# Gated linear attention in a decoder trunk: split logits and norms, Silu from Exp and Ln, heads closed at other points, another bank for the first key

## The chip, the cores and the metric

The kernel runs on one core of a Trainium2 chip. The time is the device time of one execution in microseconds (us), lower is better; three runs of the kernel before gave a median of 1874.64 us (1874.52 to 1875.6). Engines are named as in the profile: PE is the matrix engine and PEld its weight loads, DVE the vector engine, ACT the scalar engine (activation functions), POOL the general-purpose engine, SP the engine whose queue issues the weight DMAs. The matrix engine's results land in PSUM, eight banks of 128 partitions x 512 fp32; everything else lives in SBUF.

## The reference

512 tokens of width 1024 pass two layers. Each layer is a half-step SwiGLU, a mixer, another half-step SwiGLU, all behind RMSNorms. Layer 0 mixes by gated linear attention (GLA), layer 1 by stick-breaking attention. The change is in the GLA mixer only:

```
proj = h @ w_in                                  # q 512, k 512, v 1024, g 1024, gk_lr 16 columns
log_a = log_sigmoid(gk_lr @ w_gk2 + b_gk) / 16   # (512, 512): the gate logits
b = cumsum(log_a)                                # per chunk, 4 heads x 128 channels
o = sum over s <= t of (q_t * exp(b_t - b_s) * k_s) v_s       # per head, 256 wide
o = rmsnorm(o, o_norm)                           # per head, over its 256 channels
y = (o * silu(g)) @ w_out
```

## The kernel before, in words

**Precision.** Nearly every product is made of parts. A tensor is cut into a high part (ACT copies it to fp32r, a form of fp32 that the matrix engine takes in one pass) and a low part (DVE subtracts the high part), and `mm3` (L66) adds high x high, low x high and high x low. The weights are cut the same way (L124 on ACT, L126 on DVE). Some products are plain fp32 instead, which the trace shows as two matmul records for each: the gate logits `ps_z<-w,ga` (L776), the cumulative sums `ps_d<-tri,la` (L789), all products inside a head, and the output norms' sums `ps_on<-osq,gT` (L908), where a column of ones in `gT` is broadcast as the stationary operand.

**The feed.** All weight products of the whole trunk stand in one list of entries (`feed.q`), each with its weights' DMA, their cutting and a generator of matmul groups. The phases pull groups from it (`feed.step`, `feed.entries`) and put their own work between. `Feed.start` cuts weights up to three entries ahead, into four buffers each of `wh` and `wl`, and loads up to six ahead on SP's queue. The order on each engine is finally set by the planner of the language, from costs of its own; it moves instructions past each other where the data allow, and where the kernel says `issue_after` it keeps that order.

**The GLA phase** (`GLA.run`, L945). `two_halves` runs q of heads 0 and 1 (kept in PSUM, `defer`, because the RMSNorm's factor `R` isn't there yet), `stats_a` makes the row sums, `gate_low` (L763) the 16 gate columns (`ps_gk`), `stats_b` (L391) broadcasts `R` (`ps_R`, then the copy L405). Then `flush` evacuates q0 and q1 (L721), `gate_logits` (L769) scales the gate columns (L770), makes the four logit tiles (L776), and takes log-sigmoid as Abs, Exp, Ln on ACT (L778 to L780) and min-minus on DVE (L781) into `la`. Two entries, k0 and k1, follow; then `decay` (L786) makes b of heads 0 and 1.

PSUM is shared out by tags: two banks "a", three "z", two "t", one "o". All features of the mixer (q, k, g; L702, L705, L713) and v use "a"; "o" holds the small transposes, state updates and norm sums of a head.

Then come four heads. `levels(h)` (L793) builds the 128 x 128 decayed scores of head h in seven halvings: for each, DVE forms two differences of b (L811, L812), ACT takes Exp, DVE multiplies k and q on (L814, L815), PE multiplies (`ps_S`, L839) and DVE copies under a mask into `S` (L840). `output(h)` (L850), interleaved with the levels of the next head, decays the keys (`kd`), transposes them (`ps_kd`), updates the states (`ps_s`, L880 to L887), makes the output (`ps_o`), squares it (L901, L905), sums it over 256 channels by the product with ones (`ps_on`), and computes 1/rms as Exp(-0.5 Ln) with a correction step (L910 to L920) and the scaled output `on` (L924). One feed step stands between any two steps of these.

The eight gate features g are evacuated as `gn = ps * R` (L736) as they come; in the program, Silu on them (`silu`, L930) stands after all features of the phase and is followed by the load of the activation table that has Exp and Ln (L427). Only then `close(g)` (L936) is called for heads 0, 1 and 2: `on * gn`, cut into `oh` and `ol`; head 3 is closed at the end. The last two entries (`back`, L227, body L260) are the product with `w_out`: two halves of four output tiles each, where the parts of head 3 (`late=2`) come last in each half.

The gate weights are set up at the phase's start on POOL (`gate_weights`, L738): `w2` is zeroed, `w_gk2` is loaded twice, the bias once at partition 64 beside a row of ones in `ga`.

Of the kernel before, what the change touches and what calls it, by code (L numbers as in the profile page):

```python
# [10 lines left out]
F32 = mybir.dt.float32  # L11
# [21 lines left out]
def decoder(ctx: ExitStack, tc: tile.TileContext, a: dict, out: bass.AP):  # L33
# [100 lines left out]
    class Feed:  # L134
# [17 lines left out]
            e = self.q[i]  # L152
            return e.body(e.W)

        def step(self, n=1):
            while n > 0:
                if self.cur is None:
                    self.cur = self.start()
                if next(self.cur, self) is self:
                    self.cur = None  # L160
                else:
                    n -= 1
# [21 lines left out]
    def feat(ch, f, evac, tag=None, defer=None):  # L184


        def body(W):
            (wh, wl), = W
            ps = psum("ps_f", tag)
            for part in (range(0, KD // 2), range(KD // 2, KD)):  # L190
                for k in part:
                    mm3(ps, wh[:, k], wl[:, k], st["h"][k], st["l"][k], k == 0, k == KD - 1)
                if part[-1] == KD - 1:
                    if defer is None:
                        evac(ps)
                    else:
                        defer.append((evac, ps))
                yield

        feed.q.append(Entry([(ch, lambda t: t[:, :, f * P : (f + 1) * P], KD, P)], body))  # L200
# [492 lines left out]
    class GLA:  # L693
        def __init__(self, w_in, w_gk2, b_gk, og, w_out, nxt):
            self.w_in, self.w_gk2, self.b_gk, self.og = w_in, w_gk2, b_gk, og
            self.defer = []
            self.q, self.k, self.b, self.v = [None] * 4, [None] * 4, [None] * 4, []
            self.gn, self.on, self.hs = [None] * KD, [None] * KD, []
            chunks = [Chunk(cols(w_in, c * 256, 256), KD, 256) for c in range(4)]

            def qk(h):
                feat(chunks[h // 2], h % 2, lambda ps: self.evac_q(h, ps), "a", self.defer if h < 2 else None)  # L702

            def kk(h):
                feat(chunks[2 + h // 2], h % 2, lambda ps: self.evac_k(h, ps), "a")  # L705

            qk(0), qk(1), kk(0), kk(1), qk(2), qk(3), kk(2), kk(3)
            for c in range(4):
                tok(w_in, 1024 + c * 256, lambda i, ps, c=c: self.evac_v(c, i, ps), "a")
            for c in range(4):  # L710
                ch = Chunk(cols(w_in, 2048 + c * 256, 256), KD, 256)
                for f in range(2):
                    feat(ch, f, lambda ps, j=2 * c + f: self.evac_g(j, ps), "a")  # L713
            back(w_out, 0, KD, self.hs, 1.0, nxt, late=2, tags=("a", "a", "z", "z", "z", "t", "t", "o"))
# [19 lines left out]
        def evac_g(self, j, ps):  # L734
            self.gn[j] = self.gp.tile([P, T], F32, tag="g", name="gn")
            nc.vector.tensor_tensor(out=self.gn[j], in0=ps, in1=st["R"], op=ALU.mult)  # L736

        def gate_weights(self):  # L738

            gr = self.ep.tile([P, KD, 16], F32, tag="gr", bufs=1, name="gr")  # L740
            with nc.allow_non_contiguous_dma("gate columns"):
                nc.gpsimd.dma_start(gr, cols(self.w_in, 3072, 16))
            self.gs = gs = self.ep.tile([P, KD, P], F32R, tag="gs", bufs=1, name="gs")
            nc.gpsimd.memset(gs.bitcast(F32), 0.0)
            nc.scalar.copy(gs[:, :, 0:16], gr)
            nc.vector.tensor_tensor(
                out=gs[:, :, 32:48], in0=gr, in1=gs[:, :, 0:16].bitcast(F32), op=ALU.subtract
            )
            self.w2 = w2 = self.gp.tile([P, T], F32, tag="g", name="w2")
            nc.gpsimd.memset(w2, 0.0)  # L750
            nc.gpsimd.dma_start(w2[0:16], self.w_gk2)
            nc.gpsimd.dma_start(w2[32:48], self.w_gk2)
            nc.gpsimd.dma_start(w2[64:65], self.b_gk)
            self.tri = self.ep.tile([P, P], F32, tag="tri", bufs=1, name="tri")
            nc.gpsimd.dma_start(self.tri, a["c_tri"])
            lf = self.ep.tile([P, len(LEVELS) * P // 2], F32, tag="e", name="lf")
            nc.gpsimd.dma_start(lf, a["c_lvl"])
            self.lvl = self.ep.tile([P, len(LEVELS) * P // 2], U8, tag="lvl", bufs=1, name="lvl")
            nc.vector.tensor_copy(self.lvl, lf)
            self.ga = self.gp.tile([P, T], F32, tag="g", name="ga")  # L760
            nc.gpsimd.memset(self.ga[64:65], 1.0)

        def gate_low(self):  # L763
            self.psg = psum("ps_gk", "z")
# [2 lines left out]
                mm(self.psg, self.gs[:, k], st["l"][k], False, k == KD - 1)  # L767

        def gate_logits(self):  # L769
            nc.vector.tensor_tensor(  # L770
                out=self.ga[0:64], in0=self.psg[0:64], in1=st["R"][0:64], op=ALU.mult
            )
            self.la = []
            for i in range(NT):
                ps = psum("ps_z", "z")
                mm(ps, self.ga[0:65, i * P : (i + 1) * P], self.w2[0:65], True, True)  # L776
                t = self.gp.tile([P, T], F32, tag="g", name="la")
                nc.scalar.activation(t, ps, AF.Abs)  # L778
                act(t, t, AF.Exp, scale=-1.0)
                act(t, t, AF.Ln, bias=1.0)  # L780
                nc.vector.scalar_tensor_tensor(  # L781
                    out=t, in0=ps, scalar=0.0, in1=t, op0=ALU.min, op1=ALU.subtract
                )
                self.la.append(t)
# [65 lines left out]
        def output(self, h):  # L850
# [40 lines left out]
            for vb in range(2):  # L891
                ps = psum("ps_o", "t")
                c0 = h * 256 + vb * P
                for i in range(NT):
                    s = slice(i * P, (i + 1) * P)
                    mm(ps[:, s], v[i][:, c0 : c0 + P], S[:, i], True, i == 0)
                    if i > 0:
                        mm(ps[:, s], sts[i - 1][:, vb * P : (vb + 1) * P], eb[:, s], False, True)
                po.append(ps)
                t = ep.tile([P, T], F32, tag="e", name="osq")  # L900
                nc.scalar.activation(t, ps, AF.Square)  # L901
                if vb == 0:
                    sq = t
                else:
                    nc.vector.tensor_tensor(out=sq, in0=sq, in1=t, op=ALU.add)  # L905
                yield
            ps = psum("ps_on", "o")
            mm(ps, ones, sq, True, True)  # L908
            vv = ep.tile([P, T], F32, tag="e", name="vv")
            nc.vector.tensor_scalar(  # L910
                out=vv, in0=ps, scalar1=1.0 / 256, scalar2=EPS, op0=ALU.mult, op1=ALU.add
# [15 lines left out]
                self.on[j] = t  # L927
            yield

        def silu(self):  # L930
            for j in range(KD):
                with tc.issue_after(st["last"]):
                    s = nc.scalar.activation(self.gn[j], self.gn[j], AF.Silu).ins
            exp_ln_tables(s)

        def close(self, h):  # L936
            for j in (2 * h, 2 * h + 1):
                nc.vector.tensor_tensor(out=self.on[j], in0=self.on[j], in1=self.gn[j], op=ALU.mult)
                hh = self.gp.tile([P, T], F32R, tag="g", name="oh")
                hl = self.qp.tile([P, T], F32R, tag="q", name="ol")  # L940
                nc.scalar.copy(hh, self.on[j])
                nc.vector.tensor_tensor(out=hl, in0=self.on[j], in1=hh.bitcast(F32), op=ALU.subtract)
                self.hs.append((hh, hl))

        def run(self):  # L945
            with ExitStack() as es:
# [17 lines left out]
                self.decay(0)  # L964
                self.decay(1)
                prev = None
                for h in range(4):
                    if h == 1:
                        self.decay(2)
                        self.decay(3)  # L970
                    for n, _ in enumerate(self.levels(h)):
                        feed.step(1)
                        if prev is not None and n >= 1:
                            next(prev, None)
                            if n == 4:
                                feed.step(1)
                    if prev is not None:
                        for _ in prev:
                            feed.step(1)
                    prev = self.output(h)  # L980
                    if h == 3:
                        while feed.pos < self.end:
                            feed.step(1)
                        feed.finish()
                        next(prev)
                        self.silu()
                        for g in range(3):
                            self.close(g)
                for n, _ in enumerate(prev):
                    if n < 6:  # L990
                        feed.step(1)
                self.close(3)
                feed.entries(self.end + 2 - feed.pos)


# [331 lines left out]
```

## Time and profile before

| what | value |
|---|---|
| three timed runs, median | 1874.64 us |
| the profiled execution, time | 1874.33 us |
| the profiled execution, span from first to last instruction | 1872.2 us |
| granted TensorE clock | 0.998 |
| PE busy, share of span | 1847.3 us, 99% |
| DVE busy | 1412.0 us, 75% |
| ACT busy | 1012.5 us, 54% |
| POOL busy | 7.3 us |
| DMA, mean over the span | 96 GB/s |

The profile is of one execution. Its time is 2.1 us more than its span, and 0.3 us under the median of the runs. The GLA phase lies between about 354 us (the first q product) and 598 us (the first product of the next SwiGLU) of the span. "Chain of waits" below means the profile's chain of work that ended last, shown in order of time: start, length, what ran. A group line gives line, engine, operation, result and operands, shapes and count, then busy time and mean ns of one, then the idle time before.

### The profile page before, as it was taken

The numbers are of one execution on the slowest core, as the hardware profiler recorded it, in microseconds if no ns is written. First come the engines' busy times: TensorE is split into PE (matmuls) and PEld (weight loads), VectorE is DVE, ScalarE is ACT, GpSimd is POOL, SyncE is SP. The second block draws the span as 40 slices with busy tenths as digits, with TensorE's granted clock in tenths as the row PEclk, the third lists the DMA queues.
The fourth block names the chain that finished last, engine by engine and source line by source line (L and its number), as shares of the span: only waits on it lengthen the run. The fifth ranks groups of instructions, "written<-read, shape, count | busy, mean of one in ns | idle before, by whom it ended". The sixth has DMA issues, their size and how long they took to land.

```text
span 1872.2 us, 29140 instructions
## 1 busy us (share of the span) xinstructions
PE 1847.3 (99%) x11933; PEld 1650.8 (88%) x11933; DVE 1412.0 (75%) x2177; ACT 1012.5 (54%) x1714; POOL 7.3 (0%) x17
## 2 busy tenths in 40 slices
PE   8999999999999999999999999999999999999998
PEld 6899999789888899999888999998888788999997
DVE  7977776775767987777788777676878769777775
ACT  6544545444555554454555545445878755554454
POOL 0000000100000000000000000000000000000000
PEclk9999999999999999999999999999999999999999
DMA  5433333212123233342233333233221223333321
GB/s 158 130 107 110 105 113 103 87 48 66 61 75 113 79 102 102 107 129 80 79 113 116 111 102 113 79 92 101 68 68 57 68 90 113 102 102 102 119 85 68
DMA packets 177513, 179.04 MB, mean 96 GB/s; under 512 B 4034, under 2 KB 167924, under 8 KB 177380
## 3 DMA queue, kind: packets, MB, share of 16 engines
q1 hardware_dynamic: 176768, 176.18, 30.0%
q8 instruction: 93, 1.52, 0.3%
q0 software_dynamic: 512, 0.99, 0.2%
q14 instruction: 40, 0.33, 0.1%
q10 hardware_dynamic: 100, 0.03, 0.0%
HBM read 175.11 MB, written 2.10 MB: 95 GB/s over the span
## 4 chain that ended last, share of the span: by engine, by line
PE 88%; DVE 9%; ACT 1%; issue 1%; DMA 0%; SPq 0%; DVEq 0%; ACTq 0%
PE ps_d L64 25%; PE ps_w L523 20%; PE ps_f L64 11%; PE ps_q L523 10%; PE ps_z L523 5%; PE ps_t L64 5%; PE ps_b L64 4%; DVE wl L126 2%; PE ps_S L64 1%; PE ps_z L1058 1%; PE ps_bt L64 1%; DVE ts L615 1%; DVE xn L599 1%; DVE nl L606 1%; PE ps_oT L1120 1%; PE ps_T L1105 1%
## 5 line engine op out<-in xcount | busy, mean ns | idle before, releaser
L126 DVE TENSOR_TENSOR wl<-raw,wh 128x1024 fp32r<-128x1024 f32 x244 | 259.9, 1066 | 96.6 <-ACT wh L124 61.5
L124 ACT CAST wh<-raw 128x1024 fp32r<-128x1024 f32 x244 | 224.7, 923 | 131.2 <-PE ps_f L64 44.4
L64 PE MATMUL ps_d<-hh,wl 128*128 128x512 f32 x672 | 262.4, 390 | 0.0
L64 PE MATMUL ps_d<-hh,wh 128*128 128x512 f32 x672 | 262.3, 390 | 0.0
L64 PE MATMUL ps_d<-hl,wh 128*128 128x512 f32 x672 | 261.6, 389 | 0.0
L523 PE MATMUL ps_w<-th,wl 128*128 128x256 f32 x864 | 239.1, 277 | 5.0 <-DVE wl L126 5.0
L523 PE MATMUL ps_w<-tl,wh 128*128 128x256 f32 x864 | 239.0, 277 | 0.9 <-DVE tl L606 0.9
L523 PE MATMUL ps_w<-th,wh 128*128 128x256 f32 x864 | 239.2, 277 | 0.2
L307 DVE SCALAR_TENSOR_TENSOR x<-ps_d,x 128x512 f32<-128x512 f32 x184 | 124.9, 689 | 115.9 <-PE ps_d L64 115.6
L126 DVE TENSOR_TENSOR wl<-s,wh 128x1024 fp32r<-128x1024 f32 x144 | 176.1, 1223 | 40.7 <-PE ps_z L523 19.3
L124 ACT CAST wh<-s 128x1024 fp32r<-128x1024 f32 x144 | 151.2, 1050 | 93.2 <-PE ps_q L523 30.0
L124 ACT CAST wh<-rawd 128x1024 fp32r<-128x1024 f32 x84 | 88.4, 1053 | 201.7 <-issue 98.9
L64 PE MATMUL ps_f<-xh,wh 128*128 128x512 f32 x448 | 182.1, 407 | 1.6 <-DVE q L721 1.5
L64 PE MATMUL ps_f<-xl,wh 128*128 128x512 f32 x448 | 175.5, 392 | 0.0
L64 PE MATMUL ps_f<-xh,wl 128*128 128x512 f32 x448 | 175.0, 391 | 0.0
L523 PEld LDWEIGHTS ps_w<-th,wl 128*128 128x128 f32 x864 | 162.3, 188 | 5.8 <-DVE wl L126 5.8
L523 PEld LDWEIGHTS ps_w<-tl,wh 128*128 128x128 f32 x864 | 162.2, 188 | 1.1 <-DVE tl L606 1.1
L523 PEld LDWEIGHTS ps_w<-th,wh 128*128 128x128 f32 x864 | 162.2, 188 | 1.0 <-ACT wh L124 1.0
L64 PEld LDWEIGHTS ps_d<-hl,wh 128*128 128x128 f32 x672 | 126.2, 188 | 26.7
L64 PEld LDWEIGHTS ps_d<-hh,wh 128*128 128x128 f32 x672 | 126.2, 188 | 24.5
L64 PEld LDWEIGHTS ps_d<-hh,wl 128*128 128x128 f32 x672 | 126.2, 188 | 23.8
L126 DVE TENSOR_TENSOR wl<-rawd,wh 128x1024 fp32r<-128x1024 f32 x84 | 102.9, 1225 | 53.6 <-ACT wh L124 40.1
(248 smaller groups left out, 4434.4 us busy)
## 6 DMA issues: line engine op xcount, KB each, us to landing
raw<-in_ffn_w_gate_dram SPq DMA_DIRECT2D x43, 1024.0 KB, 5.3
raw<-in_ffn_w_up_dram SPq DMA_DIRECT2D x43, 1024.0 KB, 5.4
rawd<-in_ffn_w_down_dram SPq DMA_DIRECT2D x84, 512.0 KB, 3.5
raw<-in_gla_w_in_dram SPq DMA_DIRECT2D x12, 1024.0 KB, 5.5
raw<-in_sb_w_in_dram SPq DMA_DIRECT2D x16, 512.0 KB, 3.8
raw<-in_gla_w_out_dram SPq DMA_DIRECT2D x4, 1024.0 KB, 5.0
raw<-in_sb_w_in_dram SPq DMA_DIRECT2D x4, 1024.0 KB, 5.3
raw<-in_sb_w_out_dram SPq DMA_DIRECT2D x4, 1024.0 KB, 5.0
```

The costliest lines, as they stand in the source:

```text
L64: st["pe"] = nc.tensor.matmul(ps, l, r, start=first, stop=last).ins
L124: st["cut"] = nc.scalar.copy(h, r).ins
L126: nc.vector.tensor_tensor(out=l, in0=r, in1=h.bitcast(F32), op=ALU.subtract)
L307: nc.vector.scalar_tensor_tensor(out=xs[k], in0=ps, scalar=0.5, in1=xs[k], op0=ALU.mult, op1=ALU.add)
L523: st["pe"] = nc.tensor.matmul(o, l_, r_, start=first and j + n == 0, stop=j == 3 and n == 2, skip_group_check=True).ins
L599: nc.vector.scalar_tensor_tensor(out=t, in0=xs[k], scalar=g, in1=st["R"], op0=ALU.mult, op1=ALU.mult)
L606: nc.vector.tensor_tensor(out=l, in0=t, in1=h.bitcast(F32), op=ALU.subtract)
L615: nc.vector.tensor_tensor(out=o, in0=p, in1=q, op=ALU.subtract)
L1058: nc.tensor.matmul(o_, l_, r_, start=first, stop=last, skip_group_check=True)
L1105: nc.tensor.transpose(ps[:, c0 : c0 + P], ys[yb][:, yc + j * P : yc + (j + 1) * P], ident)
L1120: nc.tensor.matmul(po[e * 64 : e * 64 + 64, j * P : T], self.v[j][:, c : c + 64], self.wt[p, e][bk][:, c0 : c0 + n], start=j == 0, stop=j ...
```

## The change

Four edits, all in `class GLA` but for one argument in `Feed.step`.

1. **First key.** k0 takes the bank "o" instead of an "a".
2. **Logits by parts.** `w2` is copied to fp32r on 128 partitions (`w2r`): w_gk2 four times, the bias at two partitions; the last 32 partitions hold the low part (ACT copy, DVE subtraction). `ga` becomes fp32r with high part, low part and high part again, so that one product of 128 partitions gives high x high, low x high and high x low. It is made by one DVE product (`gl`), an ACT copy, a DVE subtraction and another ACT copy, where one DVE product made it before. POOL zeroes/sets whole tiles and issues six DMAs for `w2` where it issued three.
3. **Norm sums by parts.** The squares are cut into `sh` (ACT) and `sl` (DVE), and two fp32r products with a ones column of fp32r replace one fp32 product.
4. **Silu and closing.** Each g feature gets its Silu right after its evacuation, as g * exp(min(g, 0) - ln(1 + exp(-|g|))): Abs, Exp, Ln on ACT, one DVE operation, Exp on ACT, one DVE product. `silu()` with its table switch goes. A head is closed as soon as its output and its two gates are there, checked after each feed step of the phase, with the feed stopped at the phase's last entries until then.

The diff, cut to its core:

```diff
@@ Feed
-        def step(self, n=1):
+        def step(self, n=1, end=None):
             while n > 0:
                 if self.cur is None:
+                    if self.pos == end:
+                        return
                     self.cur = self.start()
@@ GLA
-                feat(chunks[2 + h // 2], h % 2, lambda ps: self.evac_k(h, ps), "a")
+                feat(chunks[2 + h // 2], h % 2, lambda ps: self.evac_k(h, ps), "o" if h == 0 else "a")
...
             nc.vector.tensor_tensor(out=self.gn[j], in0=ps, in1=st["R"], op=ALU.mult)
+            s = self.ep.tile([P, T], F32, tag="s", bufs=2, name="sg")
+            nc.scalar.activation(s, self.gn[j], AF.Abs)
+            act(s, s, AF.Exp, scale=-1.0)
+            act(s, s, AF.Ln, bias=1.0)
+            nc.vector.scalar_tensor_tensor(
+                out=s, in0=self.gn[j], scalar=0.0, in1=s, op0=ALU.min, op1=ALU.subtract
+            )
+            act(s, s, AF.Exp)
+            nc.vector.tensor_tensor(out=self.gn[j], in0=self.gn[j], in1=s, op=ALU.mult)
+            self.gates = j + 1
...
-            nc.gpsimd.dma_start(w2[0:16], self.w_gk2)
-            nc.gpsimd.dma_start(w2[32:48], self.w_gk2)
-            nc.gpsimd.dma_start(w2[64:65], self.b_gk)
+            for r in range(0, P, 32):
+                nc.gpsimd.dma_start(w2[r : r + 16], self.w_gk2)
+            for r in (48, 112):
+                nc.gpsimd.dma_start(w2[r : r + 1], self.b_gk)
+            self.w2 = self.gp.tile([P, T], F32R, tag="g", name="w2r")
+            nc.scalar.copy(self.w2, w2)
+            low = slice(96, P)
+            nc.vector.tensor_tensor(out=self.w2[low], in0=w2[low], in1=self.w2[low].bitcast(F32), op=ALU.subtract)
+            one = self.ep.tile([P, 64], F32R, tag="one", bufs=1, name="one")[:, 0:1]
+            nc.scalar.copy(one, gT[:, 50:51])
+            self.ones = one.to_broadcast([P, P])
...
-            nc.vector.tensor_tensor(
-                out=self.ga[0:64], in0=self.psg[0:64], in1=st["R"][0:64], op=ALU.mult
-            )
+            ga, t = self.ga, self.ep.tile([P, T], F32, tag="e", name="gl")
+            nc.vector.tensor_tensor(out=t[0:48], in0=self.psg[0:48], in1=st["R"][0:48], op=ALU.mult)
+            nc.scalar.copy(ga[0:48], t[0:48])
+            nc.vector.tensor_tensor(out=ga[64:80], in0=t[0:16], in1=ga[0:16].bitcast(F32), op=ALU.subtract)
+            nc.scalar.copy(ga[96:112], t[0:16])
...
-                mm(ps, self.ga[0:65, i * P : (i + 1) * P], self.w2[0:65], True, True)
+                mm(ps, ga[:, i * P : (i + 1) * P], self.w2, True, True)
...
+            nc.scalar.copy(sh, sq)
+            nc.vector.tensor_tensor(out=sl, in0=sq, in1=sh.bitcast(F32), op=ALU.subtract)
             ps = psum("ps_on", "o")
-            mm(ps, ones, sq, True, True)
+            mm(ps, self.ones, sh, True, False)
+            mm(ps, self.ones, sl, False, True)
...
+        def step(self, n=1):
+            feed.step(n, self.end)
+            self.close_ready()
+
+        def close_ready(self):
+            while self.closed < min(self.outs, self.gates // 2):
+                self.close(self.closed)
+                self.closed += 1
@@ GLA.run, head 3
                     if h == 3:
+                        next(prev)
                         while feed.pos < self.end:
-                            feed.step(1)
+                            self.step()
                         feed.finish()
-                        next(prev)
-                        self.silu()
-                        for g in range(3):
-                            self.close(g)
+                        self.close_ready()
```

`feed.step(1)` becomes `self.step()` everywhere in the loop over heads, `self.outs` counts the heads whose output is complete, and the last `self.close(3)` becomes `self.outs = 4` and `close_ready()`. The full order on each engine, as built, is known for both kernels: on PE it is the same before the GLA phase and from the next SwiGLU on.

## The prediction

> **What bounds the kernel now.** I read the page first, then the chain of waits over the GLA phase, the matrix engine's own waits, and the busy times by stage.
>
> ```profile
> PE 1847.3 (99%) x11933; PEld 1650.8 (88%) x11933; DVE 1412.0 (75%) x2177; ACT 1012.5 (54%) x1714; POOL 7.3 (0%) x17
> ```
>
> PE is never free, so a saving on another engine is worth nothing by itself: the time falls by PE work removed and by PE waits removed, and rises by new waits. The chain over the phase's head shows both kinds:
>
> ```profile
> 369.61 0.91 PE ps_R L401 x8
> ...
> 370.54 0.70 DVE R L405
> ...
> 371.26 0.70 DVE q L721
> ...
> 372.01 1.67 PE ps_f L64 x6
> 373.68 2.58 PE ps_z L64 x6
> 376.26 1.38 PE ps_f L64 x6
> 377.64 1.10 PE ps_z L64 x2
> 378.74 8.19 PE ps_f L64 x36
> 386.93 1.78 PE ps_d L64 x16
> ```
>
> From 370.51 to 372.01 PE stands still: k0 needs an "a" bank, and both hold q0 and q1 until L721. Then four logits take 2.58 + 1.10 = 3.68 us, two records each (0.46 us a record in this chain), while the 36 fp32r products take 8.19 / 36 = 0.2275 each. PE's waits of the whole span that lie in this phase:
>
> ```profile
> PE ps_f L64 <- DVE q L721: 1.5, 1, 1.5
> ...
> PE ps_o L64 <- DVE on L924: 0.6, 1, 0.6
> PE ps_b L64 <- ACT oh L941: 0.6, 1, 0.6
> ```
>
> The last two stand at 546 and 549 us, where heads 0 to 2 are closed late. For the stretch from the first g product to there (columns: length, then busy PE, PEld, DVE, ACT, POOL):
>
> ```profile
> 481.62:546.00 64.38, 64.34 (x355) 54.03 (x353) 41.75 (x79) 39.72 (x51) 0.00 (x0) 1.00 0.21 66
> ```
>
> PE is full; DVE has 22.6 us to spare, ACT 24.7. The clock column is 1.00 and DMA 0.21, so neither is in play.
>
> **The change, part by part.** The base is the profiled execution's 1874.33 us (span 1872.2 + 2.1), 0.3 under the median of the runs.
>
> *First key and logits.* In the order as built, PE goes from the gate columns through one k0 product and `ps_R` straight on with k0; logits come after 20 products of k0 and in k1. From the end of `ps_R` (370.52) to `ps_d` stand 48 feature products and 4 logits, 52 x 0.2275 = 11.83 us: `ps_d` starts at 382.35 instead of 386.93, **-4.6** (the wait 1.5, logits 3.68 - 0.91 = 2.8, 0.3 of restart). What is late next is `la`. The gate columns now pass DVE (0.67), ACT copy (0.6), DVE (0.67) and then PE, so logits can start at 372.6 + 2.2 = 374.8; PE reaches them at about 375.1. The log-sigmoids took 7.2 us from the first Abs to the last `la` (374.58 to 381.81). Now the first Abs starts near 375.6, one weight cut of 1.05 stands among them on ACT (383.85), and on DVE the last `la` stands behind k1's evacuation, which waits for k1 (382.4). PE does the other `ps_d` and one `ps_S` first (1.6 us, to 383.95). Hidden, barely; bounds 0 and +0.6 (k1's evacuation, 0.7, added behind 383.85), I take **+0.2**.
>
> The set-up hides: POOL issues three more DMAs (0.5 each), ending near 358.6; the ACT copy of `w2` stands behind a weight cut that waits for PE until 362.3 in both kernels, and DVE's subtraction and `lvl` fit before `rv` at 365.81 (the cut ends at 364.6; 0.6 + 0.4). Without that cover `rv`, and with it `R`, would be late by up to 0.7; behind `rv` on DVE stand only weight cuts and the norm chain.
>
> *Norms.* One row carries it:
>
> ```profile
> L64 PE MATMUL ps_on<-osq,gT 128*128 128x512 f32 x8 | 4.4, 631 | 0.1
> ```
>
> In the chain the four norms take 1.13, 1.02, 1.02 and 0.86 = 4.03 us of PE; two fp32r products each are 8 x 0.2275 = 1.82: **-2.2**. A broadcast ones column as fp32r weights isn't in the trace; bounds are 0.2275 and the fp32 record's 0.5 a product (4.0, no gain); the 188 ns load is the same for both types in the rows, so I take the first. The added cut (ACT 0.6, DVE 0.7) delays the sums by 1.3 us; in the order 16 v products of 256 columns (1.9 us) and 9, 10 and 12 products of 512 (2.0, 2.3, 2.7) stand ahead of the first part, about as long as squares, sum and cut take (0.6 + 0.7 + 0.6). No charge.
>
> *Silu.* On PE nothing. ACT loses the tables:
>
> ```profile
> L432 ACT ACT_TABLE_LOAD x7 | 9.0, 1283 | 0.9 <-DVE e L812 0.8
> ...
> L933 ACT ACT_TABLE_LOAD x5 | 6.4, 1283 | 0.1
> ```
>
> The planner had scattered the Silus, so 12 loads stand in the stage (a 13th follows): -15.4 us, and in the new order none. Seven Silus go (-4.4), eight times Abs, Exp, Ln, Exp come (0.58 + 3 x 0.63 = 2.47 each, +19.8), two cuts of squares and five of closed heads (+4.2): 39.7 becomes 43.9 us, of 63.3. ACT isn't the bound. The load at 540.22 ends at 541.50 and the next Exp starts at 541.51, so the trace has 1.28 us a switch. The Trainium skill (ScalarE: Activation LUTs, "What ACT_TABLE_LOAD costs") budgets about 2.66 us a switch, with a drain; by it the loads would be 32 us and ACT still freer. No row shows the drain, and by either the sum on PE is the same.
>
> DVE: 16 operations of 128x512 come. Neighbours without a dependence start 0.61 apart though 0.69 long:
>
> ```profile
> 504.12 0.69 DVE L918 TENSOR_TENSOR vv<-vv,y 128x512 f32<-128x512 f32 x1
> 504.73 0.42 DVE L815 TENSOR_TENSOR e<-e,q 128x256 f32<-128x256 f32 x1
> ```
>
> So +9.8, two cuts of squares +1.2, eight closing operations that stood after 546 +4.9, head 2's normalising, earlier, +2.2: 41.75 becomes 59.9 us of 63.3 (64.4 less two norms' 1.1), **95% full**. This is where a gain can be lost. The order shows the planner's answer: between head 3's identity product and its first level it puts 45 feature products (10.2 us) where 24 stood (5.45). In that time DVE must do, from `vv` on: g1 0.6, four differences 1.35, S 0.6, kd 0.5, a weight cut 1.15, vv, y and two `on` 2.9, two gate operations 1.2, two closing operations 1.2, two products on e 0.7: 10.2 us, begun about when PE ends that identity product. So PE and DVE meet there with nothing left over, and each further us on DVE is one on PE. Bounds: 0, and +4.4: DVE waits in order for Ln, for y2 and for the second Exp; the `la` waits (0.83, 0.84, 0.49 without the first; row below) give 0.72 each, three there and three again at the third level. I take **+0.8**, near the low end, since the later levels of the old order had 1.2 to 7 us between e's last product and its use.
>
> ```profile
> DVE la L781 <- ACT la L432: 5.9, 4, 3.7
> ```
>
> *Closing.* Heads 0 and 1 are closed before the w_out products begin, so both waits at 546 and 549 go: **-1.2**. Late next: head 2, whose cuts come behind DVE's backlog while PE has only 21 other w_out products (4.8 us); 0 to +1, I take **+0.3**. Head 3's chain met PE to within 0.09 us before (575.42); it gets about 3 us shorter (its key copy waited from 546.0 to 549.88 behind Silus and a table load) and PE comes some 2.7 us earlier: covered, no charge.
>
> Past the phase the order on PE is the old one. **Sum**: -4.6 + 0.2 - 2.2 + 0.8 - 1.2 + 0.3 = -6.7, **1867.6 us**.
>
> **The rivals.**
>
> *1. DVE paces the gate stage.* For it: 95% full, and in order. Against: PE's waits are 3 us in the whole phase before, with DVE as full between 503 and 526. Price: the upper bounds of the stage and of head 2, +4.4 + 1.0 instead of +1.1: 1874.33 - 6.7 + 4.3 = 1871.9. The Trainium skill (VectorE: DVE Perf Modes, "The DRAIN you can't avoid") says that the next operation doesn't start until the pipe is empty, duration less 0.27 us later; 18 new operations would cost 0.42 more each, 7.6 us, DVE 67.5 against 63.3, +4.2, much the same time. The 0.61 us starts above speak against it where nothing depends.
>
> *2. Slower: ACT's queue holds the levels.* Each gate puts four ACT operations in one queue with weight cuts that wait for PE to free a buffer, and the levels' Exp behind those.
>
> ```profile
> ACT wh L124 <- PE ps_f L64: 24.6, 13, 5.2
> ```
>
> That is 1.9 us a time. If such a wait comes between each gate's operations and an Exp that PE needs next, eight gates cost 15.1: 1867.6 + 15.1 - 1.1 = 1881.6. It cancels the gain from 7.8 us on, four such waits. Against: in this stage before, cuts waited too (4.6 us ahead of the one at 528.75), and PE waited for no Exp.
>
> *3. The change doesn't do what it says:* fp32r products with these operands run at the fp32 record's 0.46 to 0.5. Logits +1.0, norms +2.2: 1870.8. Against: every weight product of the trunk runs at 0.2275 with the same load time.
>
> **How the numbers follow.** Forecast 66%: its own range is 1865.8 (all charges at 0 give 1866.3, less half the spread of the runs, 1.1) to 1869.8. Rival 1 20%, anywhere from there to its full price; rival 2 7%; rival 3 7%. The range 1865.6 to 1872.2 takes in the forecast, rival 1 and rival 3. 0.2% is 3.7 us, about what a measurement here can tell from no change: faster means under 1870.9, slower over 1878.4. Faster: the forecast, half of rival 1 and half of rival 3, 0.80. Slower: most of rival 2, 0.06. The rest, 0.14, is the same.
>
> **What would show it.** Right: `ps_d` starts 4.4 to 4.6 us earlier, counted from `ps_gk`; PE doesn't wait for q's evacuation; the norm sums' records are near 390 ns; no table load between the phase's first and the next SwiGLU's; DVE over 90% busy in the gate stage. Wrong: waits of PE on `e`'s product or on ACT's Exp in head 3's levels adding up to over 3 us (rival 1), weight cuts on ACT followed by late Exps (rival 2), fp32r records over 0.4 us apart (rival 3).

## The result, and the profile after

Five runs of the changed kernel took 1867.43 us in the median (1866.12 to 1868.46), five of the kernel before 1874.64 (1874.13 to 1876.18): ratio 0.9961, interval 0.9949 to 0.9972. The profiled execution took 1868.2 us. The first line of its page, and its busy times:

```profile
span 1866.2 us, 29172 instructions
...
PE 1843.4 (99%) x11929; PEld 1650.5 (88%) x11929; DVE 1425.0 (76%) x2199; ACT 1012.5 (54%) x1733; POOL 8.8 (0%) x20
```

PE lost 3.9 us of busy time and the span 6.0: the rest is waiting that went. ACT is as busy as before in total, because 13 table loads of 1.283 us went where 24 activations and eight copies were added. The chain of waits over the phase's head, of the changed kernel (start, length, what ran):

```profile
366.05 3.83 PE ps_gk L64 x16
369.88 0.23 PE ps_f L64
370.12 0.89 PE ps_R L403 x8
371.01 4.34 PE ps_f L64 x19
375.35 0.80 PE ps_z L64 x3
376.16 3.20 PE ps_f L64 x14
379.36 0.30 PE ps_z L64
379.65 3.20 PE ps_f L64 x14
382.85 1.34 PE ps_d L64 x12
```

After `ps_R` PE goes straight on: the 1.5 us in which it stood still before are gone, and four logits take 0.80 + 0.30 = 1.10 us in place of 3.68. `ps_d` comes 16.80 us after `ps_gk` (382.85 - 366.05), where it was 386.93 - 365.78 = 21.15.

The waits of PE in the changed kernel, over the whole span:

```profile
PE ps_g L1285 <- DMA gl<-in_gla_o_norm_dram: 6.1, 1, 6.1
PE ps_w L525 <- DVE wl L126: 5.0, 4, 1.4
PE ps_x L1292 <- DMA x<-in_x_dram: 1.7, 4, 0.6
PE ps_w L525 <- DVE tl L608: 0.9, 1, 0.9
...
```

The columns are total, times and longest; the lines left out are of 0.4 us and less. None of them lies in the GLA phase: the three of before went and no new one came. The gate stage, from its first g product to the first product with `w_out` (length, then busy PE, PEld, DVE, ACT, POOL with counts, then clock, DMA share, GB/s):

```profile
476.88:540.23 63.35, 63.35 (x353) 53.89 (x353) 52.77 (x97) 38.12 (x64) 0.00 (x0) 1.00 0.16 52
```

DVE is busy 52.8 of 63.35 us, 83%, and not 95%.

For the experiments I cut the phase by the starts of PE's records. **H** (head) runs from the first `ps_gk` product to the first feature product after the decay's sums; **G** from there to the next SwiGLU's `ps_R`; **F** from that `ps_R` to the next one, a stretch that is the same in every kernel. Before: H 23.73, G 220.14, F 339.65. After: H 19.46, G 216.66, F 341.00. So the phase gained 4.27 + 3.48 = 7.75 us, more than the time did. Of the rest, 0.27 us was lost ahead of `ps_gk` (the first DMA wait is 6.1 us, was 5.8), and 1.35 us came back in F, in one place (busy times by stretch, columns as above):

```profile
644.80:645.20 0.40, 0.35 (x1) 0.35 (x2) 0.40 (x1) 0.40 (x1) 0.00 (x0) 0.50 0.56 141
645.20:648.00 2.80, 2.80 (x15) 2.80 (x15) 2.80 (x4) 0.45 (x2) 0.00 (x0) 0.51 0.49 166
648.00:649.00 1.00, 1.00 (x10) 1.00 (x10) 0.94 (x3) 0.00 (x0) 0.00 (x0) 1.00 0.00 0
```

The third number from the end is the granted clock. Within the second of two short waits that PE has in both kernels (0.88 us until 642.51, 0.89 until 644.85) the clock fell to a half for 3.4 us; in the kernel before it did not. Run e8 below shows that this isn't a fixed part of the changed kernel.

### The profile page after: what moved, and what is told of

The parts are those of the page before. It is cut to its first block, busy times and chain, and to the rows that moved or that the text cites. A ratio compares the mean times of both kernels' runs of the same rounds, so it can differ in the third digit from the quotient of the medians.

```text
span 1866.2 us, 29172 instructions
## 1 busy us (share of the span) xinstructions
PE 1843.4 (99%) x11929; PEld 1650.5 (88%) x11929; DVE 1425.0 (76%) x2199; ACT 1012.5 (54%) x1733; POOL 8.8 (0%) x20
## 4 chain that ended last, share of the span: by engine, by line
PE 91%; DVE 7%; ACT 1%; issue 1%; DMA 0%; DVEq 0%; ACTq 0%
PE ps_d L64 25%; PE ps_w L525 21%; PE ps_f L64 13%; PE ps_q L525 10%; PE ps_z L525 5%; PE ps_t L64 5%; PE ps_b L64 5%; PE ps_S L64 1%; DVE wl L126 1%; PE ps_z L1095 1%; PE ps_bt L64 1%; PE ps_oT L1157 1%; DVE ts L617 1%; PE ps_T L1142 1%; DVE xn L601 1%; DVE nl L608 1%
```

## The experiments

Twelve kernels, each timed beside the kernel before, whose own median was 1874.27 us beside e1 to e4, 1873.83 beside e5 to e8 and 1873.51 beside e9 to e12; so the ratios are to be compared, and the medians only within a group. Median (number of runs), ratio with its interval, then from the profile H, G and PE's waits in the GLA phase:

| run | kernel | median | ratio | H | G | waits |
|---|---|---|---|---|---|---|
| - | before | 1874.64 (5) | 1 | 23.73 | 220.14 | 1.5, 0.6, 0.6 |
| - | changed | 1867.43 (5) | 0.9961 [0.9949, 0.9972] | 19.46 | 216.66 | none |
| e1 | before + bank | 1872.44 (11) | 0.9991 [0.9982, 0.9999] | 21.95 | 220.17 | 0.7, 0.6 |
| e2 | before + logits | 1871.58 (11) | 0.9986 [0.9978, 0.9995] | 21.04 | 220.09 | 1.5, 0.6, 0.6 |
| e3 | before + norms | 1878.15 (9) | 1.0021 [1.0012, 1.0031] | 23.70 | 225.04 | 4.3, 1.5, 0.8, 0.2 |
| e4 | before + Silu and closing | 1872.09 (11) | 0.9988 [0.9979, 0.9997] | 23.71 | 217.87 | 1.5 |
| e5 | before + bank, logits, norms | 1873.56 (11) | 0.9998 [0.9989, 1.0007] | 19.46 | 224.79 | 4.3, 0.8 |
| e6 | changed, Silu by its table | 1871.04 (11) | 0.9983 [0.9974, 0.9991] | 19.49 | 219.27 | 1.4, 1.1 |
| e7 | changed, +16 DVE operations | 1873.43 (11) | 0.9998 [0.9989, 1.0007] | 19.42 | 224.00 | 3.7, 0.6, 0.2 |
| e8 | changed, again | 1866.23 (5) | 0.9959 [0.9945, 0.9973] | 19.46 | 216.78 | none |
| e9 | changed, heads closed late | 1868.05 (7) | 0.9970 [0.9959, 0.9981] | 19.45 | 217.93 | 1.1 |
| e10 | changed, +8 DVE operations | 1867.51 (5) | 0.9966 [0.9954, 0.9979] | 19.46 | 218.24 | 1.2 |
| e11 | changed, norms from the high part | 1864.83 (5) | 0.9954 [0.9941, 0.9966] | 19.46 | 215.31 | none |
| e12 | e6 with the old norm sums | 1870.87 (11) | 0.9982 [0.9973, 0.9990] | 19.44 | 219.81 | 0.8, 0.8 |

The expectations call G "C", or in e3 and e4 take a stretch that ends at the next SwiGLU's first product, 12.2 us ahead of G's end. H, G, F and the waits are of one execution each, which in e6 and e12 took 1.6 and 1.8 us less than the median, in e2 1.6 and in e3 1.1 us more; there G and the medians give different prices.

The theory at the start was the prediction's: four edits whose gains add up, and engines beside PE that have room. Its rivals: an edit that pays only in another's company, and a DVE or ACT that paces PE.

### e1: the bank alone

```diff
-                feat(chunks[2 + h // 2], h % 2, lambda ps: self.evac_k(h, ps), "a")
+                feat(chunks[2 + h // 2], h % 2, lambda ps: self.evac_k(h, ps), "o" if h == 0 else "a")
```

> Only the first key's product moves to a bank of its own; logits, norm sums, Silu and closing are as before. The theory of the prediction: the 1.5 us in which TensorE waited for q's evacuation goes, and nothing behind it waits instead, so the stretch from the gates' low-rank product to the decay's first product falls from 21.15 to about 19.6 us, and the time by 1.5 us (ratio 0.9992). Rival: the wait only moves to the next user of one of these banks, and the stretch stays within 0.3 us of 21.15. A time that differs by another 1.3 to 1.4 us should come with one more or one less stretch of about 3.4 us at half clock, and not from this stretch.

H fell by 1.78 us (to the decay's first product 19.36 us, 21.13 before), and G stayed: the wait of 1.5 with its restart, and nothing behind it. The rival falls.

### e2: the logits alone

```diff
-                mm(ps, self.ga[0:65, i * P : (i + 1) * P], self.w2[0:65], True, True)
+                mm(ps, ga[:, i * P : (i + 1) * P], self.w2, True, True)
```

(and the parts of `w2` and `ga` as in the change)

> Only the logits' products are made of parts; the rest is as before. The theory: four products of 0.91 us each in two records become four of 0.23 us, so the same stretch falls by 2.8 us to about 18.3 us; the wait for q's evacuation (1.5 us) stays; the time falls by 2.8 us (ratio 0.9985). Rival: the added cut of the low-rank product on VectorE and ScalarE makes the logits late, TensorE waits for it, and the stretch falls by less than 1.5 us. A second rival: the gain in this stretch of the two edits is not a sum, because the longer run-up hides the 1.5 us wait; then this one falls by over 4 us alone and the bank's move by nothing.

H fell by 2.69 (to the decay's first product 18.45 us), and the wait for q stayed at 1.5. Both edits together give 4.27 (e5, changed), the single ones 1.78 + 2.69 = 4.47: they add up to within 0.2. Its F was 341.17, with a half-clock stretch at 650 us.

### e3: the norm sums alone

```diff
+            nc.scalar.copy(sh, sq)
+            nc.vector.tensor_tensor(out=sl, in0=sq, in1=sh.bitcast(F32), op=ALU.subtract)
-            mm(ps, ones, sq, True, True)
+            mm(ps, self.ones, sh, True, False)
+            mm(ps, self.ones, sl, False, True)
```

> Only the output norms' sums are made of parts; the rest is as before. The prediction's term was -2.2 us (two records of 0.5 us each become two of 0.23 to 0.4 for each of four heads). The trace of the changed kernel showed only 0.40 and 0.39 us less between the last and the next level's product of heads 0 and 1, so about -1.6 us if all four heads gain alike (ratio 0.9991). Rival: heads 2 and 3 gain nothing, because the sums there are followed by other work that waits or because the cut of the squares makes the sum late: then -0.8 us or nothing. The stretch after the decay's products to the next SwiGLU's first product was 207.94 us before.

Neither: the edit alone costs 4.9 us in G, and the time rose by 0.2% (3.9 us by the medians). The chain of waits of e3 where the output products should begin:

```profile
538.84 0.35 PE ps_on L64
539.19 0.47 PE ps_f L64 x2
539.66 0.25 PE ps_on L64
...
540.18 1.06 ACT wh L124
...
542.55 0.63 ACT y L432
...
543.20 1.28 ACT L432
...
545.56 1.28 ACT L941
...
546.85 0.63 ACT gn L941
...
548.52 1.28 ACT L427
...
549.82 0.63 ACT oh L949
...
550.49 6.40 PE ps_b L64 x16
```

The sum itself is shorter (0.35 + 0.25 against 1.02), but ends 1.1 us later, since its second part waits for the cut. Now a weight cut (1.06) and a table load (1.28, like the pieces at L432, L941 and L427) stand between the sum and its Ln, which starts at 542.55 where it had started at 539.57 (that load had run at 536.21, ahead of the sum); two Silus with two more switches follow before the closing copy `oh`, which all of `ps_b` waits for. `oh` began at 545.87 before, here at 549.82. And then 16 products take 6.40 us in place of 16 x 0.2275 = 3.64, because behind the wait of 4.3 us the clock was down (busy times by stretch, the clock third from the end):

```profile
549.00:555.80 6.80, 5.31 (x13) 4.16 (x14) 6.73 (x11) 5.53 (x9) 0.00 (x0) 0.50 0.00 0
```

Wait 3.7 us longer, another of 0.8, and 2.8 from the clock, less the norms' own gain of 1.2 (below) and 0.4 of the other wait, is 5.7; 4.9 were measured.

### e4: Silu and closing alone

```diff
-                        self.silu()
-                        for g in range(3):
-                            self.close(g)
+                        self.close_ready()
```

(with Silu in `evac_g` and the other lines of the change's fourth part)

> Only Silu by Exp and Ln and the heads' early closing; bank, logits and norm sums as before. The prediction's term was -1.2 us (two waits of 0.6 us for the closing heads go, nothing is lost in the gate stage); from the changed kernel's trace, whose stretch after the decay is 3.48 us shorter, of which the norms' sums would account for 1.6, this part should give 1.9 us. Expected: that stretch at 206.0 to 206.7 us (207.94 before), time -1.2 to -1.9 us (ratio 0.9990 to 0.9994). Rival 1 of the prediction, VectorE paces the gate stage: the stretch is over 207.9 us and TensorE waits in it.

G fell by 2.27, both closing waits are gone and nothing waits in the gate stage: rival 1 of the prediction falls for this kernel. The gain is above the 1.2 that the wait table promised. In the kernel before, PE's timeline shows why; the brackets hold the idle time and who ended it:

```profile
545.47 0.49 PE L873 MATMUL ps_kd<-ident,kd 128*128 128x128 f32 x3
546.53 0.50 PE L64 MATMUL ps_b<-oh,wh 128*128 128x512 f32 x1 [0.57 <-ACT oh L941]
...
548.26 0.39 PE L64 MATMUL ps_b<-oh,wl 128*128 128x512 f32 x1
549.28 1.21 PE L64 MATMUL ps_o<-S,v 128*128 128x128 f32 x6 [0.63 <-DVE on L924]
```

The idle time is counted from the modelled end of the record ahead. Counted from start to start, three `ps_kd` took 1.06 us where they take 0.31 in e4, and the `ps_b` product 1.02 where it takes 0.23: 0.75 + 0.79 = 1.54 lost, and 0.7 more in the `ps_o` and `ps_s` behind the second wait.

### e5: all but Silu and closing

(e1, e2 and e3 together)

> Bank, logits by parts and norm sums by parts together, with Silu and closing as before. The theory: the parts add up, -1.5 -2.8 -1.6 (norms as the changed kernel's trace shows them) = about -5.9 us, up to -6.7 with the prediction's norm term of 2.2; the two waits of 0.6 us of the closing heads remain. Rival: the gains of bank and logits overlap, so that the sum of the single edits is over what both give.

The head gained its 4.27 us and G lost 4.65, with the same wait of 4.3 as e3 and the same 6.8 us at half clock: 0.9998, no difference. The first three edits without the fourth are worth nothing. That the norm edit pays only in company is a rival that the prediction didn't have.

### e6: Silu by its table, heads closed early

```diff
-            nc.scalar.activation(s, self.gn[j], AF.Abs)
...
-            nc.vector.tensor_tensor(out=self.gn[j], in0=self.gn[j], in1=s, op=ALU.mult)
+            st["gsilu"] = nc.scalar.activation(self.gn[j], self.gn[j], AF.Silu).ins
```

> The changed kernel, but with Silu by its own table, issued for each gate as it is ready; heads are still closed early. It puts 13 table loads (1.283 us each, 16.7 us) and 8 Silu (0.63 us, 5 us) on ScalarE in place of 32 Exp, Ln and Abs (0.625 us, 20 us), and takes 16 operations of 0.685 us (11 us) off VectorE. Theory, that TensorE alone sets the end here and neither engine paces it: within 0.5 us of the changed kernel's time, the gate stage (first gate product to first output product) within 0.5 us of 63.32. Rival: a table load in front of a level's Exp makes the level late; TensorE waits 0.3 us or more at several levels of heads 2 and 3, and the time is 2 us or more above the changed kernel's. Rival on the other side: VectorE's 11 us fewer shorten the gate stage, which would show that VectorE paced it.

The first rival holds in the main: G is 2.5 us above the changed kernel's (mean of two, 216.72), with two waits of PE, 1.1 for one level's operand and 1.4 for head 3's output `on`. By the medians the price is 4.8 us (1871.04 against 1866.23 of e8, timed in the same group); where the other 2.3 lie, this profile doesn't show. ACT was no fuller than 70% in the gate stage (44.8 of 64.4 us): it is not the sum of the loads that costs, but a load ahead of an Exp that a level or a norm needs. DVE, 8 us less busy, gave nothing back. Here is ACT's timeline ahead of each wait, and PE's line at its end (`y<-vv` is the norm's Ln, `y<-y` at L434 its Exp, `e<-e` the level's Exp):

```profile
499.32 0.63 ACT L434 ACTIVATE y<-vv 128x512 f32<-128x512 f32 x1
...
500.48 1.28 ACT L434 ACT_TABLE_LOAD   x1
501.78 0.63 ACT L434 ACTIVATE y<-y 128x512 f32<-128x512 f32 x1
502.31 0.62 ACT L434 ACTIVATE e<-e 128x512 f32<-128x512 f32 x1
...
504.66 0.53 PE L64 MATMUL ps_S<-e 128*64 128x64 f32 x6 [1.12 <-DVE e L834]
...
565.66 0.63 ACT L434 ACTIVATE y<-vv 128x512 f32<-128x512 f32 x1
566.31 1.28 ACT L434 ACT_TABLE_LOAD   x1
567.61 0.63 ACT L434 ACTIVATE y<-y 128x512 f32<-128x512 f32 x1
...
571.75 0.47 PE L64 MATMUL ps_b<-oh,wh 128*128 128x512 f32 x1 [1.38 <-DVE on L948]
```

e6 has 18 table loads in the phase, 15 of them in the gate stage, where 13 were expected. On the way to each wait stands a load of 1.28 us between a Ln and the next Exp, with no Silu between them. The kernel before loaded the one table that has both (L427) behind its Silus, and e6 has no such load in its place. So the two waits may be the price of Ln and Exp in separate tables, more than that of Silu's own. No run here loads the common table behind each Silu, and so this rival stays open.

### e7 and e10: more work on DVE

```diff
+            for _ in range(3):
+                nc.vector.scalar_tensor_tensor(
+                    out=s, in0=self.gn[j], scalar=0.0, in1=s, op0=ALU.min, op1=ALU.subtract
+                )
```

(in e10 `range(3 if j % 2 else 1)`; it replaces the single operation)

> The changed kernel with the middle operation of each Silu on VectorE done three times in place of once (the second undoes the first, so the value is the same but for rounding): 16 more operations of 0.689 us, 11 us, of which 14, 9.6 us, fall into the gate stage, where VectorE was busy 53.4 of 64 us. So VectorE would be 63 of 64 us busy. If TensorE is held only once VectorE is really full: 0 to +1 us. By the prediction's rival 1 (held once VectorE is at some 95%): +2 to +5 us, with TensorE waiting for VectorE in the levels of heads 2 and 3. If VectorE paced the changed kernel already: +9 us or more.

> As the kernel with the Silu's middle operation three times, but for four of the eight gates only: 8 more VectorE operations of 0.689 us, 5.5 us in place of 11, which had cost 7.3 us in C (224.00 against 216.7), with one stretch at half clock worth some 1.6 of it. So VectorE would be busy some 58 to 59 of 64 us in the gate stage. If every added operation is paid for in proportion: C at 220 or more. If VectorE holds TensorE only when it is full (the theory): C within 1 us of 216.7. The prediction's rival 1 (paid from some 95% full on) says the same as the theory here; a price of 2 us or more would put the bound at or under 90%.

16 operations (11 us) cost 7.3 us in G, 8 operations (5.5 us) 1.5. DVE's share of the gate stage hardly rose, to 55.5 of 63.65 us (87%) and 54.4 of 64.8 (84%): the work was pushed behind, into the stretch where head 2's output has to be normalised and closed. The 1.5 lies between what the theory (within 1 us) and its rival (2 or more) allowed. DVE doesn't pace PE by being full. Its order does, as DVE's timeline of e10 (start, length, line; idle time before in brackets) ahead of PE's one wait (1.2 us, for the gate's evacuation L739) shows:

```profile
523.32 1.22 DVE L126 TENSOR_TENSOR wl<-raw,wh 128x1024 fp32r<-128x1024 f32 x1
526.28 0.69 DVE L969 TENSOR_TENSOR ol<-on,oh 128x512 fp32r<-128x512 f32 x1 [1.74 <-ACT oh L968]
526.89 0.68 DVE L739 TENSOR_TENSOR gn<-ps_f,R 128x512 f32<-128x512 f32 x1
```

DVE stands idle for 1.74 us, waiting for ACT's closing copy (which stands behind a weight cut), while the evacuation that frees PE's bank is queued behind it. In e7 the waits sum to 4.5 us, and in a half-clock stretch of 6.8 us PE was busy for 5.6, half of which, 2.8, is lost: together the 7.3. So the changed kernel has room for less than 5.5 us on DVE in this stage, though by its share of busy time it has 10.6.

### e8: the changed kernel again

> The changed kernel again, with nothing altered, in the same job. Its five runs lay between 1866.12 and 1868.46 us, and the profiled one of 1868.2 us had one stretch of 3.413 us at half clock some 55 us after the linear attention that the kernel before did not have, worth 1.36 us. Theory: the spread is that stretch (or others like it): a profiled run without it has the next SwiGLU's end 7.5 us earlier than before, not 6.1, and a time near 1866.3 to 1866.9; with it, near 1868. Rival: the stretch is there in every run, and the spread comes from somewhere else, such as the first load of the span.

H and G are the first profile's to within 0.12 us, but F is 339.54: no half-clock stretch at the two waits of 0.9 us, although both are there. The span is 1864.0 and not 1866.2. Across all profiles F is 339.5 to 339.7 in seven kernels without such a stretch (before, e1, e3, e4, e5, e10, e11) and e8, and 340.9 to 341.2 in the three with it (the first profile of the changed kernel, e2, e9): 1.4 us. (e6 and e12 have one more wait for a weight cut there, 340.1 and 339.8; e7, at 338.8, has one wait of 1.35 in place of the two.) The granted clock agrees: the runs of e8 at 0.999 took 1865.34 to 1866.23, those at 0.998 took 1866.99 and 1867.08.

### e9: heads closed late

```diff
             feed.step(n, self.end)
-            self.close_ready()
```

> The changed kernel with Silu by Exp and Ln, but the first three heads closed only after the last gate, as before. C is the stretch from the first feature product after the decay's sums to the next SwiGLU's broadcast of row scales: 220.14 us before, 216.66 and 216.78 changed, 219.27 with Silu by its table and early closing. Theory: the table loads were the price and the place of closing is worth little: C within 0.7 us of 216.7. Rival: the closing of three heads (12 operations of 0.69 us on VectorE, 6 of 0.62 on ScalarE, 8.3 us on the fuller engine) lands between the last gate and the first output product, where only head 3's levels are left to cover it: C at 218 to 220 us, with TensorE waiting for a closing copy or for head 3's norm.

G 217.93, 1.2 above the changed kernel's: between both. The rival's mechanism is there, but small, and on ACT: PE waits 1.1 us for `kt`, a copy of head 3's keys that stands behind ACT's weight cut. The early closing is worth some 1.2 us beside Silu by Exp and Ln; beside Silu by its table it is worth 224.79 - 219.27 = 5.5 (e5 against e6, alike in the other three edits), the place of the Silus and the common table's load, which differ too, included.

### e11: norm sums of the high part only

```diff
-            mm(ps, self.ones, sh, True, False)
-            mm(ps, self.ones, sl, False, True)
+            mm(ps, self.ones, sh, True, True)
```

> The changed kernel, but the output norms' sums use only the first of the two parts of the squares; the low part, its cut on VectorE and its product on TensorE are left out, so the sums are rounded. Theory: in the trace of the changed kernel the two products of a head take 0.50 and 0.25 us on TensorE's chain where the kernel before took 1.13 for its two records; without the low part C falls by 4 x 0.25 = 1.0 us to about 215.7, and the time by 1.0. Rival: the order of the other work around it fills or opens gaps, and C moves by less than 0.3 or by more than 2.

G fell by 1.4 us, 1.0 expected from the four products. It has the lowest time of all, 0.9954, but it leaves out the low part of the squares and so rounds the norms' sums; its interval overlaps that of e8. Whether the last 0.4 us are the cut on DVE or the order around it, it doesn't tell.

### e12: Silu by its table with the old norm sums

(e6, with e3's edit taken back)

> The changed kernel with Silu by its own table, heads closed early, and the norms' sums by one fp32 product as before (no cut on ScalarE). Theory from the runs so far: norms by parts cost 4.9 us in C beside Silu by table and late closing, and gain 1.2 beside Silu by Exp and Ln, because the cut puts 0.63 us more on ScalarE's queue and on the way to the norm, where table loads of 1.283 us stand. Then without the cut the table form is within 1 us of Exp and Ln without the cut: C at 217.5 to 218.9 (217.87 there), no wait of TensorE over 0.6 us. Rival: the loads cost 2.6 us whether the cut is there or not, C at 220 us or more.

My theory fell: without the cut G is 219.81, 1.9 above e4's 217.87 and not within 1, with two waits of 0.8. So against this form of the table, without the common one loaded again, Exp and Ln are worth 1.9 us with the old norm sums and 2.5 with the new, in G of one profile each; the cut is not what makes the difference. What ruins the cut in e3 and e5 is the late closing together with its table switches (without the switches, e9, late closing costs 1.2): the norm edit gains 1.2 us beside Exp and Ln (217.87 to 216.72), 0.5 beside the table with early closing (219.81 to 219.27), and loses 4.9 beside the table with late closing.

## Why the prediction was right, and where its steps were off

The forecast was 1867.6 us, its range 1865.6 to 1872.2; 1867.43 was measured. That agreement is partly luck: the phase gained 7.7 us (4.27 + 3.48, e8 4.27 + 3.36) where the sum had 6.7. The norms' term was 1.0 us too large and that of closing 1.1 too small, which cancel; the three charges, 1.3 together, did not come; and 1.6 us of the profiled execution were lost again outside the phase (0.27 ahead of it, 1.35 at half clock). Against the kernel before timed beside them, the first five runs gained 7.2 us and those of e8 7.6. Of the signs that were named, two did not come though the time did: norm records near 390 ns (446 and 432), and DVE over 90% busy (83%). Step by step:

- **First key and logits**, -4.6 with a charge of +0.2: right. H -4.27, `ps_d` 4.35 us earlier counted from `ps_gk` (4.4 to 4.6 was the sign); bank 1.78, logits 2.69. PE doesn't wait for `la`, and the set-up stayed hidden.
- **Norms**, -2.2: the mechanism right, the size not. The products' time on PE's chain fell from 4.03 to 2.39 us (0.75, 0.62, 0.46, 0.56 by head), not to 1.82, and G by 1.2. The chain around head 0's sum in the changed kernel:

```profile
452.39 0.53 DVE osq L932
...
452.94 0.63 ACT sh L936
...
453.61 0.50 PE ps_on L64
454.11 0.47 PE ps_t L64 x4
454.58 0.25 PE ps_on L64
```

The second product of a pair takes 0.25, near the 0.2275 assumed. The first takes 0.50 here, where it follows a product of 256 columns and the cut is just done; with feature products around it (e3 at 538.84) 0.35. The groups of instructions give 446 and 432 ns a record (mean ns behind the busy time), but records of successive products overlap, and this is not what a product costs:

```profile
L64 PE MATMUL ps_on<-sh,one 128*128 128x512 f32 x4 | 1.8, 446 | 0.1
L64 PE MATMUL ps_on<-sl,one 128*128 128x512 f32 x4 | 1.7, 432 | 0.0
```

"No charge" for the cut held only with the other edits: in e3 the same cut costs 4.9 us net.
- **Silu**, "on PE nothing": this step failed. Against its own table at the same place the Exp and Ln form is worth 1.9 (e12) to 2.5 us (e6) in G, because of where switches stand in ACT's queue; whether the Silus' own or those between Ln and Exp, stays open. I priced ACT by its busy sum (39.7 to 43.9 of 63.3; 38.1 was measured), and the sum was not the point.
- **DVE 95% full, +0.8**: mis-sized. DVE did 97 operations in the gate stage where it had done 80, 10.3 us more and not 18.1; the rest fell behind the first output product. PE goes from 45 feature products after head 3's identity product (10.24 us, as the order said) into the levels without a wait. Charge 0.
- **Closing, -1.2 and +0.3**: with the two waits gone G fell by 2.3 (e4, where Silu changed too), of which the starts above account for 2.2, since the profile's idle column leaves out what the restart costs; head 2 is not late, charge 0.

The rivals: 1 did not occur, but e10 shows it 5.5 us of DVE work away, and e7 far beyond, set off by the order and not by the share that it named. Rival 2's mechanism is real (e3, e5, e6: PE waits for what stands behind ACT's queue), for table loads and weight cuts and not for the gates' Exps. Rival 3 is out: the logits' four products take 1.10 us.

## What to carry to other kernels

An edit that is a loss alone can be a gain beside another: three of these four edits together moved nothing, because a cut on ACT landed among table switches that the fourth removes (e3), so try the set and each part. On an in-order engine beside a full PE, price not the busy share but the queue: what stands ahead of the one instruction that PE needs next, and what that one waits for. And take a wait's price from start to start on the waiting engine, since idle time counted from modelled ends showed only 1.2 of some 2.2 us here.

## What the runs showed of the hardware

PE's clock fell to a half at short waits: for 3.41 us at two waits of 0.88 to 0.94 us (changed kernel, e2, e9), and for 6.83 us at a wait of 3.7 to 4.3 (e3, e5, e7), by the clock records of the traces. Single waits of 1.1 to 1.5 us (before, e2, e6, e10 and others) had no such consequence in these profiles. Here are the two waits of the changed kernel, on PE's timeline:

```profile
642.51 0.39 PE L525 MATMUL ps_w<-th,wl 128*128 128x256 f32 x1 [0.88 <-DVE wl L126]
...
644.85 0.58 PE L525 MATMUL ps_w<-tl,wh 128*128 128x256 f32 x1 [0.89 <-DVE tl L608]
```

In e8 nearly the same two waits (0.88 and 0.92) left the clock alone, and the traces show why. In each of the fourteen, all changes of the clock lie whole multiples of 3.413 us apart; in the changed kernel it fell at 644.55, rose one step later, and fell again at 1863.11, 357 steps after the first fall. So the span can be cut into such windows. In the changed kernel the first wait and 0.59 us of the second lie in one window (first line: the number behind the length is PE's busy time, the clock is third from the end); in e8 a boundary lies between the two waits (last two lines):

```profile
641.14:644.55 3.41, 1.89 (x12) 1.43 (x11) 3.38 (x5) 2.54 (x5) 0.00 (x0) 1.00 0.91 302
...
639.22:642.63 3.41, 2.48 (x19) 2.09 (x19) 3.38 (x5) 3.17 (x5) 0.00 (x0) 1.00 0.54 155
642.63:646.05 3.42, 2.50 (x22) 2.30 (x21) 3.42 (x5) 1.73 (x3) 0.00 (x0) 1.00 0.94 298
```

The Trainium skill (TensorE: Matmul & The Clock Gate, "What's actually happening") has the clock judged in a free-running window of 3413 ns, and at half speed after an idle window of about 3.4 us. The window's length and its running on agree with these traces. That a whole window has to be idle does not: in the window ahead of each short stretch PE was busy 1.89, 1.79 and 1.97 us (changed kernel, e2, e9), ahead of the long ones 0.35 to 0.57. No bound in the profile's busy time comes out, since windows with 1.90 (e2 and e4, ending near 373 us) and 1.64 (e11, ending at 1857.48) had no half clock behind them. The price is 1.4 us for the short stretch, and 2.8 in e3, where it makes a wait of 4.3 us cost 7.
